# Two norm rows, a few multiplies and four block sums of a decoder layer, moved between engines and in time

## Chip, cores and metric

The kernel runs on all 8 cores of one Trainium2 chip, two dies of four cores. Every core runs the same program on its own part of the tokens. The metric is the device time of the slowest core in microseconds. The three fast executions of the kernel before lie within 0.8 us. In some executions the cores of one die show a lower granted TensorE clock and the time is longer: in one of the kernel before, cores 0 to 3 took 1647.1 to 1666.9 us at mean granted clocks of 0.816 to 0.833, cores 4 to 7 1422.4 to 1428.5 us at 0.993 to 0.995.

## The reference, cut to what matters

```python
def _layer(x, attend_fn, conv_prev, ffn_prev, g_attn_norm, w_in, ..., w_out, g_ffn_norm, w_gate, w_up, ..., w_down):
    ...
    x = x + mixed @ w_out
    h = _rmsnorm(x, g_ffn_norm)                                   # the FFN norm row
    a, ffn_state = _causal_dwconv(h @ w_gate, ffn_prev, ffn_conv_w)
    x = x + (jax.nn.silu(a + ffn_conv_b) * (h @ w_up)) @ w_down
    return x, k, v, conv_state, ffn_state
# after the layer: y = _rmsnorm(x, g_final)                       # the final norm rows
```

A norm row is `rsqrt(mean(x*x) + eps)` over 2048 features. Features lie on partitions here, so the sum is a matmul with a matrix of ones, and the root is `exp(-0.5 * ln(...))` on ScalarE. The gate, up and down products are done as seven block products instead of eight (P1, P2, P6, P5, P7, P3, P4), which needs sums and differences of operand blocks beforehand.

## The kernel before

Three places matter. First, the FFN norm row. Each of 32 row tiles of the output projection is evicted (VectorE adds the matmul's result in PSUM to the tile in SBUF), copied with its gain into the f16 operand, squared, and added to a running sum on GpSimd:

```python
def wo_post(i):
    ...
    T.tt("dve", x2, pair(wbank(i), W), x2, ALU.add)
    T.act(hq[t][...], x2, AF.Copy, scale=col(V_GF + oc))
    if oc == 0:
        T.act(acc2[t][:, :, 0:W], x2, AF.Square)
    else:
        sq = sqw[i % 2][:, :, 0:W]
        T.act(sq, x2, AF.Square)
        if oc < 15:
            T.tt("pool", acc2[t][:, :, 0:W], acc2[t][:, :, 0:W], sq, ALU.add)
        else:
            last2[t] = sq
    ...                                   # three held stores are issued from GpSimd's queue here
def r2_calc(t, b):                        # the row of token half t
    for h in range(2):
        T.mm(psb[b + h][:, 0:W], onesf, acc2[t][:, h, 0:W], start=True, stop=False)
        T.mm(psb[b + h][:, 0:W], onesf, last2[t][:, h, :], start=False, stop=True)
    T.act(r, pair(b, W), AF.Ln, bias=epsc, scale=1.0 / D)
    T.act(pair(b, W), r, AF.Exp, scale=-0.5)
def hook0(name, u, used):                 # called after each unit of each product of the first double
    if (name, u) == ("P2", 0):
        r2_calc(1, 2)                     # TensorE needs GpSimd's last sum here
    if (name, u) == ("P6", 1):
        bg.put(hprep(1), 0.75, tag="h1")  # multiplies by the row, all on VectorE
```

The row of the first token half, `r2_calc(0, 0)`, is taken earlier, inside the output projection. A "double" is the seven block products of two column blocks, 112 matmuls in 13.8 us. Second, background work on VectorE is queued with a cost and a delay. The delay counts units, one product of one column block each. The cost (0.36 below) is what one item takes from a credit that each unit refills, so it decides how many items go out between two evictions:

```python
def after_up(p, c):
    bg.flush(("c", p, c))
    gate_mul(p, c)
    if c == 1:
        bg.put(asums(p), 0.36, delay=6, tag=("T", p))   # four block sums of a pair of gated rows
```

Third, the tail. The last down products leave 144 columns of each token half for 16 small products. The norm rows of the columns that are already done (432 per half) are taken before them, and those columns are scaled and stored beside them ("main stores", yt). Then the row of the rest is taken, and 16 "tail stores" (yz) follow:

```python
fin_calc(1, a3[1], last3[1], r3[1], psb[1][:, 0:R3T])    # row of half 1, before the first product
for oc in range(16):
    ...                                                  # 12 matmuls
    if oc == 0:
        fin_calc(0, a3[0], last3[0], r3[0], rps[0])
    T.tt("dve", x3, h2(ps), x3, ALU.add)
    ...                                                  # square on ScalarE
    if oc < 15:
        T.tt("pool" if oc < 13 else "dve", accT, accT, s_, ALU.add)
    if oc < 14:
        fin0(oc)                                         # scale row oc of the done columns, store it
fin_calc(2, accT, s_, a3[0][:, 0:R3W], rT)
fin0(14); fin0(15)
for oc in range(16):
    ...                                                  # multiply by gain and row, on VectorE
    T.dma("sp", yz_d[oc], zb[oc])
```

The softmax here doesn't subtract the row's maximum and nothing guards it: scores larger than these inputs give would overflow.

## Time and profile before

| | before |
|---|---|
| median of 4 executions, one of them slow | 1431.58 us (1430.86 to 1583.1) |
| spans of the profiled execution, fastest and slowest core | 1420.2 and 1430.1 us |
| TensorE busy on the slowest core | 97% |

### The profile page before, as it was taken

To read this page: it belongs to the slowest core of one execution; us is meant where nothing else is said; L and a number is where in the kernel's file an instruction comes from. 1 tells how busy PE (TensorE), PEld (TensorE's weight loads), DVE (VectorE), ACT (ScalarE), POOL (GpSimd) and SP (SyncE) were. 2 spreads that over 40 slices of the span, in tenths; PEclk is the share of its full clock that TensorE was granted. 3 is DMA by queue.
4 is the path that set the end of the run, shared out by engine and by line. 5 is a ranking of instruction groups with operands and counts; after the bars stand their busy time and mean duration, and the time that the engine had idled before them with its cause. 6 is when DMAs were issued, how large, how long until landed. Compare 5 with 4: busy or idle time off the path is not lost.

```text
span 1430.1 us, 27878 instructions; the slowest of 8 cores (1420.2 to 1430.1 us)
## 1 busy us (share of the span) xinstructions
PE 1383.3 (97%) x11362; PEld 1060.8 (74%) x11362; DVE 958.5 (67%) x1608; ACT 592.1 (41%) x1332; POOL 465.0 (33%) x523
## 2 busy tenths in 40 slices
PE   5999999999999999999999999999999999999996
PEld 4777777777777777777777777777777777777454
DVE  3778577887313868866767676676766665566867
ACT  4536665753333335434443433444344222222234
POOL 2002132331332304322232232223224655456445
PEclk9999999999999999999999999999999999999998
DMA  9937633355988915756665654564345988485607
GB/s 205 245 46 114 94 63 59 63 92 95 236 189 187 173 41 112 151 118 143 134 132 129 136 115 104 128 140 87 66 96 130 273 215 192 76 220 114 111 1 265
DMA packets 49201, 189.15 MB, mean 132 GB/s; under 512 B 9584, under 2 KB 16368, under 8 KB 40624
## 3 DMA queue, kind: packets, MB, share of 16 engines
q0 software_dynamic: 21376, 100.39, 42.8%
q1 hardware_dynamic: 27696, 86.98, 18.6%
q8 instruction: 89, 1.46, 0.4%
q14 instruction: 40, 0.33, 0.1%
HBM read 249.42 MB, written 40.77 MB: 203 GB/s over the span
## 4 chain that ended last, share of the span: by engine, by line
PE 81%; DVE 8%; DMA 5%; issue 2%; ACT 2%; POOL 2%; SPq 1%; DVEq 0%; POOLq 0%; ACTq 0%
PE psb L214 81%; DVE arena L239 6%; DMA arena<-xt 2%; DVE arena L258 2%; POOL arena L239 1%; ACT arena L235 1%; DMA arena<-wout 1%; DMA arena<-wg 1%; DMA arena<-wd 1%; SPq L209 1%; DMA x2s<-arena 0%; ACT arena L263 0%; PE psb L218 0%; ACT L235 0%; POOL x2s L209 0%
## 5 line engine op out<-in xcount | busy, mean ns | idle before, releaser
L214 PE MATMUL psb<-arena 128*128 128x288 f16 (+8 forms) x11290 | 1381.7, 284 | 34.2 <-DVE arena L239 14.1
L214 PEld LDWEIGHTS psb<-arena 128*128 128x128 f16 (+2 forms) x11290 | 1056.2, 99 | 354.9 <-issue 22.0
L239 DVE TENSOR_TENSOR arena<-psb,arena 128x288 f32<-128x288 f32 (+11 forms) x756 | 330.2, 455 | 330.7 <-PE psb L214 313.5
L239 POOL TENSOR_TENSOR arena<-arena 128x288 f32<-128x288 f32 (+6 forms) x378 | 389.9, 1054 | 334.4 <-ACT arena L235 215.2
L239 DVE TENSOR_TENSOR arena<-arena 128x1024 f16<-128x1024 f16 (+12 forms) x583 | 427.4, 749 | 63.0 <-ACT arena L235 32.3
L263 ACT COPY arena<-psb 128x289 f32<-128x289 f32 (+4 forms) x624 | 243.1, 407 | 532.6 <-PE psb L214 467.1
L235 ACT ACTIVATE arena<-arena 128x1184 f32<-128x1184 f32 (+17 forms) x358 | 273.3, 794 | 225.0 <-DVE arena L239 183.2
L258 DVE SCALAR_TENSOR_TENSOR arena<-arena 128x1184 f32<-128x1184 f32 (+5 forms) x140 | 181.2, 1307 | 49.9 <-ACT arena L235 47.3
L209 POOL DMA_DIRECT2D arena<-wu x22 | 11.9, 539 | 277.0 <-PE psb L214 261.8
L235 ACT ACTIVATE arena<-psb,arena 128x256 bf16<-128x256 f32 (+7 forms) x157 | 62.4, 482 | 57.1 <-PE psb L214 57.1
L209 POOL DMA_DIRECT2D arena<-win x30 | 16.5, 572 | 178.7 <-PE psb L214 169.8
L209 POOL DMA_DIRECT2D arena<-wg x22 | 12.9, 586 | 89.0 <-PE psb L214 89.0
L251 DVE TENSOR_SCALAR arena<-arena 128x256 f16<-128x256 f32 (+1 forms) x40 | 12.3, 351 | 18.3 <-DMA arena<-xt 18.3
L263 ACT COPY arena<-arena 128x32 f32<-128x32 f32 (+1 forms) x140 | 24.4, 204 | 0.0
L239 DVE TENSOR_TENSOR arena<-arena,psb 128x1156 f16<-128x1156 f16 (+2 forms) x22 | 23.4, 1104 | 0.0
L209 POOL DMA_DIRECT2D arena<-wd x32 | 18.2, 570 | 11.9 <-PE psb L214 11.9
L258 DVE SCALAR_TENSOR_TENSOR arena<-arena,psb 128x432 f32<-128x432 f32 (+1 forms) x33 | 19.2, 612 | 2.3 <-ACT psb L235 2.3
L209 POOL DMA_DIRECT2D arena<-wout x8 | 4.4, 558 | 36.0 <-PE psb L214 36.0
L265 POOL COPY arena<-arena 128x2 f32<-128x2 f32 (+1 forms) x16 | 5.5, 348 | 13.8 <-DVE arena L239 13.7
L218 PE MATMUL psb<-arena 128*128 128x128 f16 (+1 forms) x72 | 6.7, 212 | 0.0
L218 PEld LDWEIGHTS psb<-arena 128*128 128x128 f16 (+1 forms) x72 | 5.2, 97 | 1.3 <-ACT arena L235 0.2
L263 ACT CAST arena<-psb 128x256 f16<-128x256 f32 (+2 forms) x16 | 4.8, 356 | 3.2 <-PE psb L214 3.2
(17 smaller groups left out, 28.6 us busy)
## 6 DMA issues: line engine op xcount, KB each, us to landing
arena<-wg POOLq DMA_DIRECT2D x22, 1024.0 KB, 13.3
arena<-wu POOLq DMA_DIRECT2D x22, 1024.0 KB, 8.9
acs<-arena SPq DMA_DIRECT2D x16, 1008.0 KB, 5.2
arena<-acs SPq DMA_DIRECT2D x16, 1008.0 KB, 27.3
arena<-win POOLq DMA_DIRECT2D x14, 1024.0 KB, 10.4
arena<-wd POOLq DMA_DIRECT2D x16, 768.0 KB, 12.4
arena<-wd POOLq DMA_DIRECT2D x16, 640.0 KB, 8.9
arena<-x2s SPq DMA_DIRECT2D x16, 576.0 KB, 12.6
```

Source lines behind the costliest of these rows:

```text
L209: return self.add(q, lambda: eo.dma_start(out=out, in_=in_), [in_, *after], [out, *wr], dma=q)
L214: return self.add("pe", lambda: nc.tensor.matmul(out, lhsT, rhs, start=start, stop=stop, **kw), [lhsT, rhs], [out])
L218: return self.add("pe", lambda: nc.tensor.transpose(out, in_, ident), [in_, ident], [out])
L235: return self.add("act", lambda: nc.scalar.activation(out=out, in_=in_, func=func, **kw), rd, wr)
L239: return self.add(eng, lambda: eo.tensor_tensor(out=out, in0=in0, in1=in1, op=op), [in0, in1], [out])
L251: return self.add(eng, lambda: eo.tensor_scalar(out=out, in0=in0, scalar1=s1, scalar2=s2, op0=op0, **kw), rd, [out])
L258: return self.add(eng, lambda: eo.scalar_tensor_tensor(out=out, in0=in0, scalar=scalar, in1=in1, op0=op0, op1=op1), rd, [out])
L263: return self.add("act", lambda: nc.scalar.copy(out=out, in_=in_), [in_], [out])
L265: return self.add(eng, lambda: eo.tensor_copy(out=out, in_=in_), [in_], [out])
```

## The change

The intent is to give TensorE a product to do while GpSimd finishes the norm row, to unload VectorE in the first doubles, and to shorten the work behind the last product. The diff, cut to its core:

```diff
-            T.act(hq[t][...], x2, AF.Copy, scale=col(V_GF + oc))
+            hx = lambda: T.act(hq[t][...], x2, AF.Copy, scale=col(V_GF + oc))
+            if oc < 13:
+                hx()
...
+            if oc > 12:
+                hx()                      # rows 13 to 15: square first, copy after
...
+            if t == 1:
+                T.act(r, r, AF.Exp, scale=-0.5)     # a second copy of the row, in SBUF, for GpSimd
...
-            if (name, u) == ("P2", 0):
+            if (name, u) == ("P2", 1):
                 r2_calc(1, 2)
             if (name, u) == ("P6", 1):
-                bg.put(hprep(1), 0.75, tag="h1")
+                for q, k in [(2, 0), (2, 4)]:
+                    hnorm("pool", 1, q, k, k + 4)
+                bg.put(hprep(1), 0.9, tag="h1")
...
-                bg.put(asums(p), 0.36, delay=6, tag=("T", p))
+                bg.put(asums(p), 0.36, delay=22 if p == 1 else 6, tag=("T", p))
...
+        T.act(lnA[:, 0:1], epsc, AF.Ln)             # loads the logarithm's table early
...
-        fin_calc(1, a3[1], last3[1], r3[1], psb[1][:, 0:R3T])
...
             if oc == 0:
-                fin_calc(0, a3[0], last3[0], r3[0], rps[0])
+                fin_calc(1, [a3[1], last3[1]], r3[1], rps[1])    # both rows after the first product
+                fin_calc(0, [a3[0], last3[0]], r3[0], rps[0])
...
+                if oc < 13:
+                    T.tt("pool", accT, accT, sqT[oc % 4], ALU.add)
+            if oc < 10:
+                T.act(h2(zb[oc]), x3, AF.Copy, scale=col(V_GN + oc))
+            if 0 < oc < 15:
+                fin0(fq.pop(0))
+            if oc in (3, 9):
+                fin0(fq.pop(0))
+        fin_calc(2, [accT, sqT[1], sqT[2], sqT[3]], rTs, rT)     # last three squares summed by TensorE
+        T.act(rTs, rTs, AF.Exp, scale=-0.5)
+        for oc in (0, 2, 3, 1, 5, 7, 4, 8, 10, 6, 11, 12, 9, 13, 14, 15):
+            if oc < 10:
+                T.tt("pool" if oc in (1, 4, 6, 9) else "dve", zb[oc], zb[oc], ..., ALU.mult)
+            else:
+                T.stt("dve", h2(zb[oc]), rowt(oc), col(V_GN + oc), h2(rT), ALU.mult, ALU.mult)
```

More of the change, by code (lines that the diff above doesn't have):

```diff
@@ L1361, in wo_post @@
             T.tt("dve", x2, pair(wbank(i), W), x2, ALU.add)
-            T.act(hq[t][:, 2 * (oc // 8):2 * (oc // 8) + 2, oc % 8, 0:W], x2, AF.Copy, scale=col(V_GF + oc))
+            hx = lambda: T.act(hq[t][:, 2 * (oc // 8):2 * (oc // 8) + 2, oc % 8, 0:W], x2, AF.Copy, scale=col(V_GF + oc))
+            if oc < 13:
+                hx()
             if oc == 0:
@@ L1398, in hnorm @@
             v = hq[t][:, q, k0:k1, 0:W]
-            T.tt(eng, v, v, rps[t][:, q % 2].unsqueeze(1).to_broadcast([128, k1 - k0, W]), ALU.mult)
+            r = rps[t] if eng == "dve" else r2[t][:, :, 0:W]
+            T.tt(eng, v, v, r[:, q % 2].unsqueeze(1).to_broadcast([128, k1 - k0, W]), ALU.mult)
         def hsum(t, o_, a_, b_, eng="dve"):
@@ L1406, in hprep @@
         def hprep(t):
-            hn = lambda q: [lambda k=k: hnorm("dve", t, q, k, k + 4) for k in (0, 4)]
+            hn = lambda q: [lambda k=k: hnorm("dve", t, q, k, k + 4) for k in (0, 4)
+                            if t == 0 or (q, k) not in [(2, 0), (2, 4)]]
             return hn(0) + hn(2) + hn(1) + hn(3) + [
@@ L1900, in sq_acc, with fin_calc @@
                 T.tt("pool", a3[h], a3[h], s_, ALU.add)
-        def fin_calc(bank, acc, last, tmp, out):
-            ps = psb[bank][:, 0:acc.shape[1]]
-            T.mm(ps, onesf, acc, start=True, stop=False)
-            T.mm(ps, onesf, last, start=False, stop=True)
+        def fin_calc(bank, terms, tmp, out):
+            ps = psb[bank][:, 0:tmp.shape[1]]
+            for n, x in enumerate(terms):
+                T.mm(ps, onesf, x, start=(n == 0), stop=(n == len(terms) - 1))
             T.act(tmp, ps, AF.Ln, bias=epsc, scale=1.0 / D)
@@ L1931, in build_nc @@
         R3W = 2 * (576 - R3T)
-        fin_calc(1, a3[1], last3[1], r3[1], psb[1][:, 0:R3T])
-        T.act(r3[1], r3[1], AF.Exp, scale=-0.5)
         rps = [psb[h][:, 0:R3T] for h in range(2)]
@@ L1952, in build_nc, with tail_mm @@
         sqT = [x[:, 0:R3W] for x in (r3[0], sq3[0], sq3[1], sq3[2])]
+        zb = [V((O_P if i < 10 else A_OFF[4] - 10 * 1152) + i * 1152, [R3W]) for i in range(16)]
         def h2(ap):
             return ap.rearrange("p (h c) -> p h c", h=2)
-        for oc in range(16):
+        def tail_mm(oc):
             A = dA(24 + oc // 2)
@@ L1963, in build_nc @@
                 T.mm(ps, A[:, k, c0:c0 + 128], bslt[kk][:, 2 * kh:2 * kh + 2, R3T:576], start=(k == 0), stop=(k == 2 * n3 - 1))
+            return ps
+        fq = list(range(16))
+        for oc in range(16):
+            ps = tail_mm(oc)
             if oc == 0:
-                fin_calc(0, a3[0], last3[0], r3[0], rps[0])
+                fin_calc(1, [a3[1], last3[1]], r3[1], rps[1])
+                fin_calc(0, [a3[0], last3[0]], r3[0], rps[0])
+                T.act(r3[1], r3[1], AF.Exp, scale=-0.5)
             x3 = rowt(oc)
@@ L1970, in build_nc @@
             else:
-                s_ = sqT[oc % 4]
-                T.act(h2(s_), x3, AF.Square)
-                if oc < 15:
-                    T.tt("pool" if oc < 13 else "dve", accT, accT, s_, ALU.add)
-            if oc < 14:
-                fin0(oc)
-        rT = psb[2][:, 0:R3W]
-        fin_calc(2, accT, s_, a3[0][:, 0:R3W], rT)
-        fin0(14)
-        fin0(15)
-        zb = [V((O_P if i < 10 else A_OFF[4] - 10 * 1152) + i * 1152, [R3W]) for i in range(16)]
-        for oc in range(16):
-            if oc % 8 in (2, 5, 7):
-                T.act(h2(zb[oc]), rowt(oc), AF.Copy, scale=col(V_GN + oc))
-                T.tt("dve", zb[oc], zb[oc], rT, ALU.mult)
+                T.act(h2(sqT[oc % 4]), x3, AF.Square)
+                if oc < 13:
[6 more added lines that the diff above has]
+                fin0(fq.pop(0))
+        rT = psb[2][:, 0:R3W]
+        rTs = a3[0][:, 0:R3W]
+        fin_calc(2, [accT, sqT[1], sqT[2], sqT[3]], rTs, rT)
+        T.act(rTs, rTs, AF.Exp, scale=-0.5)
+        for oc in (0, 2, 3, 1, 5, 7, 4, 8, 10, 6, 11, 12, 9, 13, 14, 15):
+            if oc < 10:
+                T.tt("pool" if oc in (1, 4, 6, 9) else "dve", zb[oc], zb[oc], rTs if oc in (1, 4, 6, 9) else rT, ALU.mult)
             else:
```

## The prediction

> **What bounds the kernel now.** I read the page's busy shares first, then the list of cores, then TensorE's own timeline on all eight cores for its idle gaps, then the stretch tables around those gaps, and last the timeline of the final 40 us.
>
> ```profile
> PE 1383.3 (97%) x11362; PEld 1060.8 (74%) x11362; DVE 958.5 (67%) x1608; ACT 592.1 (41%) x1332; POOL 465.0 (33%) x523
> core 3: 1429.4 us, clock 0.994
> core 6: 1430.1 us, clock 0.993
> ```
>
> TensorE is busy 97% of core 6's span, the slowest. A change that leaves the matmuls alone can win only its idle gaps, any time at a low clock, and what comes after its last product. The second slowest core is 0.7 us behind, so a gain on core 6 alone counts only that far.
>
> TensorE's timeline after 470 us, core 6 first, then the two gaps of core 3 (start, duration, and in brackets the idle time before with its releaser):
>
> ```profile
> 488.34 82.51 PE L214 MATMUL psb<-arena 128*128 128x288 f32 x640 [2.01 <-POOL arena L239]
> 571.09 12.06 PE L214 MATMUL psb<-arena 128*128 128x289 f16 x96 [0.24 <-DVE arena L239]
> 584.00 526.00 PE L214 MATMUL psb<-arena 128*128 128x289 f16 x4236 [0.85 <-ACT arena L263]
> 1388.15 26.66 PE L214 MATMUL psb<-arena 128*128 128x432 f32 x200 [0.79 <-DVE arena L239]
> 1415.88 1.60 PE L214 MATMUL psb<-arena 128*128 128x288 f32 x4 [1.07 <-DVE arena L239]
> ...
> 570.07 12.06 PE L214 MATMUL psb<-arena 128*128 128x289 f16 x96 [0.24 <-DVE arena L239]
> 582.99 526.00 PE L214 MATMUL psb<-arena 128*128 128x289 f16 x4236 [0.85 <-ACT arena L263]
> ```
>
> The 2.01 us gap is the FFN norm row waiting for the last square sum on GpSimd. It exists on cores 6 (2.01) and 7 (2.27) only; on cores 0 to 5 VectorE runs level with TensorE there and the row finds its sum ready. The pair 0.24 + 0.85 is on cores 3, 5 and 6 only. The gap of 0.79 and the tail behind it are on all eight. Clock in stretches (the column before the DMA share) just after the first gap, cores 6 and 7:
>
> ```profile
> 488.30:489.50 1.20, 1.16 (x3) 0.91 (x4) 1.20 (x3) 0.00 (x0) 1.20 (x3) 0.50 0.93 337
> 488.00:490.00 2.00, 2.00 (x11) 1.47 (x10) 1.07 (x3) 0.09 (x1) 1.11 (x3) 1.00 1.07 310
> ```
>
> On core 6 the clock is halved after the gap, until about 491.6. On core 7, with a longer gap, it is not. Core 6 needs 676.17 us from 433.82 to 1110 where core 1, with no gap, needs 671.26: 4.9 us, which are 2.01 + 0.24 + 0.85 of gaps and about 1.9 of half clock.
>
> The tail of core 6:
>
> ```profile
> 1413.46 0.46 DVE L239 TENSOR_TENSOR arena<-arena 128x288 f32<-128x288 f32 x1 [1.05 <-POOL arena L239]
> 1415.74 0.45 DVE L239 TENSOR_TENSOR arena<-psb,arena 128x288 f32<-128x288 f32 x1
> 1418.05 0.41 ACT L235 ACTIVATE psb<-arena 128x288 f32<-128x288 f32 x1
> 1424.57 0.45 DVE L239 TENSOR_TENSOR arena<-arena,psb 128x288 f32<-128x288 f32 x1
> 1419.31 8.26 SPq L209 DMA_DIRECT2D yz<-arena  x16
> ```
>
> The last product ends at 1414.81, but VectorE evicts it only at 1415.74, since it had waited 1.05 us for GpSimd's sum. The norm row is ready at 1418.46. VectorE then makes 16 rows by 1425.02, yet SyncE issues the 16 stores one every 0.50 us, the last at 1427.22: VectorE is done 2.2 us before the last issue. The issue of the stores, not the multiplies, sets the end. The list of DMA stretches has 300 to 370 GB/s from 1414 to 1428.
>
> [...]half clock after 2.01 us idle on core 6, none after 2.27 us on core 7, so chance decides at this length. [...]a 128x1024 f16 sum takes 0.68 us alone and 2.10 us beside the GpSimd addition at 486.78, while the PSUM multiplies of the tail keep 0.65 us beside a busy GpSimd.[...]
>
> **Part 1, FFN norm row.** It moves behind one more product of 8 matmuls, 0.99 us of work that fills the gap. The squares of rows 13 to 15 go ahead of the copies, so the square of row 13 is ready 0.67 us earlier; GpSimd's chain (1.85 add, three issues of 0.55, 1.42 add) follows and ends at about 487.55 instead of 488.19. TensorE is free at 486.33 + 0.99 = 487.32. The gap falls from 2.01 to about 0.4, and the half clock should go: 1.6 + 1.9 = 3.5 us on core 6, about 1.8 on core 7, nothing elsewhere. GpSimd takes two multiplies of 1152 elements; from 1.41 us for 576 I estimate 2.8 us each, 5.6 us in all, beside VectorE's own four by then (1.35 each[...]). VectorE loses 2.7 us, but no product waited for it there: worth nothing. The half row is needed about 24 us later.
>
> **Part 2, block sums of pair 1.** Four sums of about 0.45 us leave the double in which a late weight load (13.8 us to landing) has already made VectorE late by 3.5 us. That is 1.8 us of relief against gaps of 0.24 and 0.85 us. I take 0.8 of the 1.09 on cores 3, 5 and 6. The sums land in the next double, where VectorE has some 4 us of room in 14.
>
> **Part 3, the tail.** Products first: TensorE runs 16 products of 1.48 and two norm rows of 1.46 (26.6 us) directly from 1387.36, ends at 1414.02, and gains 0.79 on every core. The table load leaves ScalarE's way, but both rows now come after one product, so the first output multiply starts at about 1395.8 (before: 1394.1). GpSimd does the same 12 additions of 0.80 and 9 multiplies of 1.13, 19.8 us, from about 1395.0 on; its last sum ends near 1414.0 and its last multiply near 1415.1. At the end VectorE has two PSUM multiplies of 0.57 per product, a little over its 1.48, so it evicts the last product at 1414.2. Then 0.45 eviction, 0.45 square, and the four terms of the row: the first three run from 1414.05 to 1415.5 (0.48 each), the last is through at 1416.2, logarithm and exponential 0.95: row ready at 1417.2 instead of 1418.46. The main stores are issued by 1417.0. First tail store at about 1417.75 (before 1419.31), then 15 steps of 0.50 instead of 7.91: last issue 1425.25 instead of 1427.22, 1.95 earlier. The multiplies shared by VectorE and GpSimd buy only the 0.4 of the steps. Against it stands the DMA: from about 1416.5 some 1.33 MB of main stores and 2.36 MB of tail stores are left, 10.2 us at 360 GB/s, so the data end near 1426.8, no sooner than the last issue needs. I take 1.7 us for the tail.
>
> **Sum.** Core 6: 1430.1 - 3.5 - 0.8 - 1.7 = 1424.1. Core 3: 1429.4 - 0.8 - 1.7 = 1426.9. So core 3 becomes the slowest, and the chip gains 3.2 us, not 6. The timed runs stand at 1431.6, so 1431.6 - 3.2 = 1428.4; since some executions will have had a core like 6 in front, I say 1428.2.
>
> **Rivals.** First, the tail stores are bound by DMA bandwidth: moving the main stores later by 1.7 us and together makes a backlog, and the earlier norm row wins nothing. For it: 0.98 to 1.00 DMA share at 1420 to 1424. Against: the last 4 us before fell to 0.84, so the issue had the lead there. Then only 0.8 to 1 us of the tail is left: 1429.2. Second, [...]the weight sums of two SBUF inputs in the first double stretch as the one from 0.68 to 2.10 did, the evictions behind them miss a slack of about 0.55 us, and TensorE gets new gaps of up to 1 us on every core: 1429. Third, the slowest core is decided by the first 60 us, where gaps for input loads differ by 3 us between cores, and a core without the removed gaps leads: gain of the tail alone, 1429.9. Fourth, the executions of before owe their time to the core with gap and half clock, and the chip gains all 6 us: 1425.8.
>
> **Range and chances.** The gains lie between 0.9 and 6 us, and there is no step that could cost more than a microsecond or two. Range 1425.8 to 1430.6. Two per cent are 28 us, more than all idle gaps and the tail together offer, so within 2% gets 0.985; a slow execution among few gives slower 0.01, faster 0.005.
>
> **What would show it.** Right: no gap over 0.6 us before the f32 matmuls near 488 and clock 1.00 behind it; no gap at 571 and 584; none before the norm rows at 1387; the last tail store issued 1.5 to 2.3 us earlier relative to TensorE's last f16 product plus 0.79; store steps of 0.50 from the first on. Wrong: a gap in the first double behind a stretched VectorE sum[...], the stores' issue running well ahead of their landing (bandwidth), or SyncE waiting for GpSimd's last multiply after the row is ready. The prediction fails as a whole if the slowest core loses time in loads that the change does not touch.

3.5 + 0.8 + 1.7 = 6.0 us for core 6, 0.8 + 1.7 = 2.5 us for core 3, so 1430.1 - 1426.9 = 3.2 us for the chip, 1428.4 for the timed runs, put at 1428.2. The 1.28 us of the table load are from the trace (core 6 at 1389.92 us). The 360 GB/s of part 3 are my estimate from stretches like 1419 to 1421 and 1420 to 1422 us, which have 362 and 370. That GpSimd's multiplies would stretch the weight sums (second rival) was my estimate, from the one sum that took 2.10 us beside a GpSimd addition and 0.68 us alone.

## More of the kernel before

To compare kernels I cut each core's span into stages at points that every run has. **Stage 1** runs from TensorE's restart near 432 us, after a short gap that all cores have, to the first eviction of 160 columns on VectorE near 520 us: the end of the output projection, the FFN norm row and the first two doubles. **Stage 2** runs from there to TensorE's restart near 1105 us: the other gate and up products. The **tail stage** runs from TensorE's restart near 1357 us to the end of the span.

## The result, and the profile after

| | before | after |
|---|---|---|
| median of 4 executions | 1431.58 us | 1428.23 us (1426.83 to 1428.63) |
| ratio after / before, fast runs | | 0.9977, 95% interval 0.9957 to 0.9996 |
| spans of the profiled execution, slowest core | 1430.1 us | 1427.6 us |
| the same, mean of the 8 cores | 1425.70 us | 1422.65 us |

The ratio is the mean time of one kernel's fast runs over that of the other's of the same rounds, so not quite the ratio of the medians. Executions in which one die ran at a lower clock are left out of the means. The median of before holds one slow execution; without it, it is 1431.52 us. The gain of 3.3 us is small but outside the noise. By stages, means of the eight cores of the two profiled executions, in us:

| | start to 432 | stage 1 | stage 2 | 1105 to 1357 | tail |
|---|---|---|---|---|---|
| before | 433.32 | 89.23 | 583.80 | 250.91 | 68.44 |
| after | 433.24 | 88.14 | 583.42 | 251.14 | 66.70 |
| difference | -0.08 | -1.09 | -0.38 | +0.23 | -1.74 |

The differences sum to -3.06 and lie in the three stages that the change touches. The cores differ more than that: after, core 3 restarts at 436.78 us and core 6 at 430.74.

The list of cores after:

```profile
core 3: 1427.6 us, clock 0.994
core 6: 1419.3 us, clock 0.996
```

Core 6, which was slowest, is now 8.3 us ahead of core 3. TensorE's timeline after, core 6 first, then core 3 from 440 us on (start, duration, in brackets the idle time before and its releaser):

```profile
430.74 670.56 PE L214 MATMUL psb<-arena 128*128 128x288 f16 x5388 [0.92 <-DVE arena L239]
1352.53 54.06 PE L214 MATMUL psb<-arena 128*128 128x432 f16 x346 [0.47 <-DVE arena L239]
...
571.11 13.04 PE L214 MATMUL psb<-arena 128*128 128x288 f16 x104 [0.48 <-DVE arena L239]
584.32 515.93 PE L214 MATMUL psb<-arena 128*128 128x289 f16 x4154 [0.17 <-DVE arena L239]
```

On core 6 the gap in front of the norm row is gone. One unbroken piece of 670.56 us takes the place of four pieces, and the tail is one piece too, without the gap of 0.79. On core 3 the gaps of 0.24 and 0.85 have become 0.48 and 0.17.

The tail of core 3 after, from the timeline:

```profile
1392.92 0.66 DVE L258 SCALAR_TENSOR_TENSOR arena<-arena,psb 128x432 f32<-128x432 f32 x1
1413.22 0.45 DVE L239 TENSOR_TENSOR arena<-psb,arena 128x288 f32<-128x288 f32 x1
1415.60 0.41 ACT L235 ACTIVATE psb<-arena 128x288 f32<-128x288 f32 x1
1418.24 2.63 DVE L258 SCALAR_TENSOR_TENSOR arena<-arena,psb 128x288 f32<-128x288 f32 x6
1416.63 8.43 SPq L209 DMA_DIRECT2D yz<-arena  x16
```

The tail stage starts 0.67 us earlier here (1360.98) than in core 6 before (1361.65), so add 0.67 to compare. The row is ready at 1416.01 + 0.67 = 1416.68 (before 1418.46). The first tail store is issued at 1417.30 (before 1419.31). VectorE is done at 1420.87 + 0.67 = 1421.54 (before 1425.02). SyncE's last issue is at 1424.72 + 0.67 = 1425.39 (before 1427.22). VectorE gained 3.5 us, the last issue 1.8, and the end of the span 1.7 (mean of all cores).

### The profile page after: what moved, and what is told of

It reads as the page before. It is cut to its first block, busy times and chain, and to the rows that moved or that the text cites. A ratio compares the mean times of both kernels' runs of the same rounds, so it can differ in the third digit from the quotient of the medians.

```text
span 1427.6 us, 27904 instructions; the slowest of 8 cores (1418.7 to 1427.6 us)
## 1 busy us (share of the span) xinstructions
PE 1380.8 (97%) x11366; PEld 1060.1 (74%) x11366; DVE 957.3 (67%) x1600; ACT 594.1 (42%) x1339; POOL 471.1 (33%) x529
## 4 chain that ended last, share of the span: by engine, by line
PE 81%; DMA 8%; DVE 7%; ACT 1%; issue 1%; POOL 1%; SPq 1%; POOLq 0%; DVEq 0%
PE psb L214 80%; DVE arena L239 5%; DMA arena<-xt 3%; DMA arena<-acs 2%; DVE arena L258 1%; DMA arena<-wout 1%; ACT arena L235 1%; DMA arena<-wg 1%; POOL arena L239 1%; SPq L209 1%; DMA arena<-wd 1%; ACT arena L263 0%; PE psb L218 0%; DVE arena L251 0%; ACT L235 0%
## 5 line engine op out<-in xcount | busy, mean ns | idle before, releaser
L239 POOL TENSOR_TENSOR arena<-arena 128x288 f32<-128x288 f32 (+8 forms) x384 | 396.2, 1054 | 338.4 <-ACT arena L235 218.5
L235 ACT ACTIVATE arena<-arena 128x1184 f32<-128x1184 f32 (+18 forms) x365 | 276.1, 788 | 220.1 <-DVE arena L239 175.3
L239 DVE TENSOR_TENSOR arena<-arena,psb 128x1156 f16<-128x1156 f16 (+2 forms) x20 | 20.4, 1081 | 4.5 <-ACT psb L235 4.5
```

The costliest lines, as they stand in the source:

```text
L235: return self.add("act", lambda: nc.scalar.activation(out=out, in_=in_, func=func, **kw), rd, wr)
L239: return self.add(eng, lambda: eo.tensor_tensor(out=out, in0=in0, in1=in1, op=op), [in0, in1], [out])
```

## The experiments

Twelve kernels ran on the chip, all with correct results. "Quiet" is a core whose VectorE is level with TensorE when the norm row comes, "late" one where it is behind.

### The norm row put back

```diff
-            if (name, u) == ("P2", 1):
+            if (name, u) == ("P2", 0):
                 r2_calc(1, 2)
-                ... hnorm("pool", ...) ...     # and the copies in front of the squares for all rows
```

> The changed kernel with the FFN norm row put back (row after the first unit of the second product, copies before squares, no multiply on GpSimd). Stage 1 is TensorE's restart near 432 us to VectorE's first 160-column eviction near 520 us; it took 88.40 us on undisturbed cores, 90.9 and 92.3 on the two with the gap before, 88.14 on all eight after. Theory: only cores where VectorE runs late show it: 88.4 on some, 90 to 92.5 on one to four of the eight, with a gap of about 2 us on GpSimd in front of the f32 matmuls. Rival (the row costs nothing and the gap of before was a chance of that execution): 88.1 to 88.4 on all eight. Tail stage stays at 66.7 +-0.15.

Stage 1 took 88.39 to 92.62 us, mean 89.96. Six of eight cores had the gap: 0.20, 0.74, 1.09, 1.29, 2.15 and 2.33 us. Two of the gaps had the length of about 2 us that I expected on one to four cores. The tail had a mean of 66.85. So the gap is no accident of one execution: with the old row it comes on two cores of eight before and on six here, at a length that changes from core to core and run to run. Core 2's gap in TensorE's timeline, and a stretch of the row behind it (the clock is the column before the DMA share):

```profile
489.85 246.34 PE L214 MATMUL psb<-arena 128*128 128x288 f32 x1960 [2.33 <-POOL arena L239]
```

```profile
491.40:493.00 1.60, 1.60 (x5) 0.87 (x5) 0.00 (x0) 0.18 (x1) 0.00 (x0) 0.50 1.18 138
```

The clock is at 0.50 again, and stage 1 is 92.62 - 88.39 - 2.33 = 1.90 us longer than gap and quiet stage explain. Behind the gap of 1.29 on core 6 the clock stayed at 1.00 and the excess was 0.24; behind the other three short gaps it was 0.23 to 0.24 too. Not expected: stage 2 was about 0.5 us longer than after on quiet cores (583.6 against 583.05), with two gaps of 0.18 waiting for ScalarE near 730 and 841 us. The kernel below with the copies in front of the squares has the same 0.55 us and two such gaps. The edit that both share is the order of copies and squares; how it acts 240 us later is open.

### The gap made longer

```diff
 # in the kernel before
+                    if i == 30:
+                        for _ in range(3):
+                            T.copy("pool", sq, sq)
                     T.tt("pool", acc2[t][:, :, 0:W], acc2[t][:, :, 0:W], sq, ALU.add)
```

> The kernel before with three copies of 576 elements on GpSimd[...] put in front of the last addition of the norm row, so that every core has a gap of some 1 to 5 us in front of the row. Theory: the gap costs more than its length: where it is longer than about 2 us, some or all cores run the eight f32 matmul passes behind it at half clock (0.48 instead of 0.24 us each, 1.9 us in all) and stage 1 is 88.4 + gap + 1.9. Rival (the half clock on core 6 was a chance and not caused by the gap): stage 1 is 88.4 + gap on all cores and the clock in the row is 1.00.

All eight cores had a gap, 2.05 to 3.42 us, and all eight ran at 0.50 behind it. Stage 1 exceeded 88.4 plus the gap by 1.76 to 1.92 us on six cores, and by 3.1 on the two with the gaps of 3.37 and 3.42 us. Core 4's gap, and the stretch behind it:

```profile
492.04 620.54 PE L214 MATMUL psb<-arena 128*128 128x288 f32 x4972 [2.05 <-POOL arena L239]
```

```profile
492.10:493.60 1.50, 1.50 (x4) 1.07 (x5) 0.35 (x1) 0.00 (x0) 1.38 (x3) 0.50 0.45 169
```

In the profiles of the kernel before, of this one and of the one with the row put back there are twelve gaps of 2 us or more in front of the row. Eleven were followed by half clock and one (2.27 us, core 7 before) was not. None of the four gaps up to 1.29 us was. In front of this row, a gap of 2 us with half clock behind it cost about 4 (2.01 and some 1.9 on core 6 before).

Which gap half clock follows is not chance in these profiles, and the traces show what separates the two kinds, though I had overlooked it. A core's clock record in the trace lists when the granted clock changes. On core 6 before it begins at 17.27 us, with changes at 27.51, 30.92, 44.57, 47.99, 488.31 and 491.72 us; the distances are 3, 1, 4, 1, 129 and 1 times 3.413 us. In the records of all cores before and after, each of the 18 stretches at half clock before the tail lasts 3.413 us, and all distances are multiples of it within 0.003 us. So I divided each core's time into steps of this measured length, starting from its own changes, and looked how much of a gap falls into one step. I take the 526 gaps over 0.9 us between 110 and 1395 us, on all cores of all profiles. In eleven of them 1.98 us or more fell into one step, and half clock followed each time. In the other 515 at most 1.91 us did, and it never followed. (The ends of TensorE's records are modelled, so the hundredths are rough.) The share in one step does not explain every half clock: on cores 0 and 3 before it also came at 218.63 and 220.80 us, for 3.413 us each, in the middle of 112.33 us in which TensorE's timeline shows no gap. The 2.27 us of core 7 are cut by the steps into 1.24 and 1.03. Even the 2.58 us of core 5 before, far from the norm row, have at most 1.87 in one step, and the clock behind them stayed at 1.00:

```profile
1170.84 4.34 PE L214 MATMUL psb<-arena 128*128 128x288 f16 x34 [2.58 <-DMA arena<-acs]
1170.84:1172.84 2.00, 2.00 (x17) 1.60 (x18) 0.13 (x1) 0.80 (x2) 0.00 (x0) 1.00 1.03 371
```

### The squares behind the copies again

```diff
-            if oc < 13:
-                hx()
+            hx()
...
-            if oc > 12:
-                hx()
```

> The changed kernel with the norm row still one product on and its GpSimd share, but the squares of rows 13 to 15 behind the copies again. On late cores the changed kernel's relatives show a gap of 0.44 us on GpSimd before the f32 matmuls, the old row 2.0 to 2.3. Theory (the product covers 0.99 us, the earlier squares the rest): a gap of 1.0 to 1.3 us and stage 1 of 89.2 to 89.6 on late cores, no half clock, 88.14 on the others. Rival (the move alone does it): 0.44 us or less on late cores, as with the squares first.

Two cores were late, with gaps of 0.55 and 1.01 us and no half clock. The relatives of the changed kernel that keep the squares in front have 0.35 to 0.45 there on late cores. One gap lies in the expected range of 1.0 to 1.3 and one below it. So, as far as two cores can say, the product in between does most of it, and the earlier squares the rest. The quiet cores showed what I had not foreseen: 88.39 us in place of 88.14. The row of the first token half, inside the output projection, also waited for its last square. The view is VectorE's, ScalarE's and TensorE's load timeline of core 1 near 447 us, before and then after; the f32 load is the row's:

```profile
446.12 0.76 DVE L239 TENSOR_TENSOR arena<-psb,arena 128x578 f32<-128x578 f32 x1 [3.20 <-PE psb L214]
448.45 3.63 PEld L214 LDWEIGHTS psb<-arena 128*128 128x128 f32 x24 [0.45 <-issue]
450.28 0.75 ACT L235 ACTIVATE arena<-psb,arena 128x578 f32<-128x578 f32 x1 [1.94 <-PE psb L214]
```

```profile
447.32 0.76 DVE L239 TENSOR_TENSOR arena<-psb,arena 128x578 f32<-128x578 f32 x1 [3.20 <-PE psb L214]
451.22 0.74 ACT L235 ACTIVATE arena<-psb,arena 128x578 f32<-128x578 f32 x1 [1.63 <-PE psb L214]
```

From the last eviction to the logarithm it is 4.16 us before and 3.90 after, and TensorE's load no longer stops for 0.45 us. That is the 0.25 us.

### The row's multiplies all on VectorE

```diff
-                for q, k in [(2, 0), (2, 4)]:
-                    hnorm("pool", 1, q, k, k + 4)
-                bg.put(hprep(1), 0.9, tag="h1")
+                bg.put(hprep(1), 0.75, tag="h1")
```

> The changed kernel with all FFN row multiplies on VectorE, none on GpSimd, the row still one product on. Theory: VectorE has room, so stage 1 stays at 88.14 +-0.1 on all cores; the GpSimd share gains nothing and costs nothing. Rival (the 0.25 us that stage 1 lost on quiet cores come from VectorE's relief): 88.3 to 88.5. Other rival[...]: stage 1 becomes shorter than 88.1.

None of the three held. Stage 1 took 88.74 us on quiet cores, 0.60 more than after, and all eight cores had a new gap of 0.33 us near 500 us. Late cores took 89.8 to 90.2. VectorE's first multiplies and the eviction behind them on core 3, and TensorE's gap:

```profile
492.21 6.41 DVE L239 TENSOR_TENSOR arena<-arena,psb 128x1152 f16<-128x1152 f16 x5 [1.40 <-ACT psb L235]
498.55 0.45 DVE L239 TENSOR_TENSOR arena<-psb,arena 128x289 f32<-128x289 f32 x1
499.05 4.18 PE L214 MATMUL psb<-arena 128*128 128x289 f16 x32 [0.33 <-DVE arena L239]
```

Five multiplies go in front of the eviction of P7, and P4 has to wait for that bank. As changed only four stand there:

```profile
493.46 5.15 DVE L239 TENSOR_TENSOR arena<-arena,psb 128x1152 f16<-128x1152 f16 x4 [2.15 <-ACT psb L235]
494.23 4.73 POOL L239 TENSOR_TENSOR arena<-arena 128x1152 f16<-128x1152 f16 x2 [4.75 <-ACT arena L235]
498.53 0.45 DVE L239 TENSOR_TENSOR arena<-psb,arena 128x289 f32<-128x289 f32 x1
```

Why this hurts only now follows from the program's order: the unit that now fills the gap in front of the row stood behind it before, and gave VectorE 1 us for the multiplies. Moved in front, it is missing there. With the row put back (above), five stood there too, and quiet cores took 88.39 us without a gap. The 0.60 us are the gap of 0.33 and 0.27 more; the short gaps with the row put back also cost 0.23 to 0.24 us more than their length.

But this run undoes two things: GpSimd's share, and the cost of a multiply in VectorE's queue, 0.75 here and 0.9 as changed. I worked the queue's rule through for both: at 0.75 it sends five multiplies ahead of P7's eviction, at 0.9 four, whether six or eight are waiting. So the higher cost alone keeps the fifth out of the way. All eight multiplies on VectorE at 0.9 were not run, so it is not shown that the GpSimd share is needed.

### The block sums put back

```diff
-                bg.put(asums(p), 0.36, delay=22 if p == 1 else 6, tag=("T", p))
+                bg.put(asums(p), 0.36, delay=6, tag=("T", p))
```

> The changed kernel with the four block sums of pair 1 back at their old place. Stage 2 is the first 160-column eviction near 520 us to TensorE's restart near 1105 us; before 583.35 on quiet cores and 584.50 on cores with the two gaps, after 583.05 and 583.66. Theory: the gaps of 0.24 (VectorE) and 0.85 (ScalarE) are back on the cores whose weight load lands late, and stage 2 is 584.2 to 584.5 there, and 583.3 on the others. Rival (the gaps went because the norm row now leaves VectorE less to do or shifts the loads): stage 2 stays at 583.0 to 583.7. Stage 1 stays 88.14, tail 66.7.

Stage 2 took 583.35 to 583.48 on five cores, 584.10 on one, and 584.49 on two, whose gaps are those of before (0.24 and 0.85). After it was 583.04 to 583.18 and 583.66 to 584.05. The theory held, and the quiet cores gain 0.3 us as well. Which wait that is can't be read from the gaps listed.

### The tail put back

The part of the diff from the early table load on was undone.

> The changed kernel with the tail of the kernel before (norm rows before the first product, no early table load, last sums on VectorE, final multiplies on VectorE only). The tail stage is TensorE's restart near 1357 us to the end of the span: 68.44 before, 66.70 after. Theory: the parts are independent, so 68.4 +-0.15 on every core with the gap of 0.79 back; stages 1 and 2 as after (88.14; 583.0 to 583.7). Rival (some of the tail's gain comes from earlier stages, such as later or earlier loads): a tail between 67 and 68.

The tail took 68.31 to 68.56 us, the gap of 0.79 was back on all cores, and stage 2 was as after. The parts are independent. Two cores were late in stage 1 (89.00 and 89.07 us), with a gap of 0.44 us: this is what the moved row leaves of the 2 us.

### The final multiplies all on VectorE

```diff
-                T.tt("pool" if oc in (1, 4, 6, 9) else "dve", zb[oc], zb[oc], rTs if oc in (1, 4, 6, 9) else rT, ALU.mult)
+                T.tt("dve", zb[oc], zb[oc], rT, ALU.mult)
```

> The changed kernel with all 16 final multiplies on VectorE and none on GpSimd, order unchanged. Theory (the issue of 16 stores at 0.50 us on SyncE sets the end, not the multiplies): VectorE needs 16 x 0.4 = 6.4 us, still faster than 16 stores in 8.1 us, so the tail stays at 66.7 +-0.15 us. Rival (the multiplies set the end, as the split on GpSimd suggests): four multiplies of 0.37 us more, tail 68.0 to 68.2 us.

The tail took 66.73 us on average (after 66.70). The third engine buys nothing: the multiplies were not what the end waited for.

### Fewer issues, and two issuing engines

```diff
 # pairs
-            T.dma("sp", yz_d[oc], zb[oc])                       # 16 times
+            T.dma("sp", yz_d[2 * n:2 * n + 2].rearrange("o p c -> p o c"), V(z, [2, R3W]))   # 8 times
 # two issuers
-            T.dma("sp", yz_d[oc], zb[oc])
+            T.dma("sp" if zn[oc] % 2 == 0 else "act", yz_d[oc], zb[oc])
```

> The changed kernel with the 16 tail stores made 8, two rows in one store, multiplies in plain order with rows 3, 5, 7 and 9 on GpSimd. If the issue on SyncE sets the end, eight issues of about 0.6 us end 3 us sooner; if the DMA engines are full, the data take as long as before (3.7 MB left at about 365 GB/s). Theory: both are near: the tail comes down from 66.7 to 65.0 to 66.0 us and the DMA share is 0.97 or more to the end. Rival 1 (issue alone): 63.5 to 64.5 us. Rival 2 (bandwidth alone): 66.5 to 66.9 us.

> The changed kernel with every other tail store issued from ScalarE's queue, 16 stores as before, same bytes and same packets. Theory: the issue is halved to about 4 us and the DMA engines become the bound: tail 65.0 to 66.0 us. Rival 1 (issue alone sets the end): 62.5 to 64 us. Rival 2 (bandwidth sets the end already): 66.5 to 66.9 us.

Both gave 66.08 us on average, 0.62 less than after and just above the expected 65.0 to 66.0. The last issue came 2.5 us earlier, and the time from it to the end of the span grew from 2.9 us to 4.7 (means of eight cores). Stretches of the DMA on core 1 with pairs (the last two columns are the share and GB/s), then core 3 after:

```profile
1411.40:1413.40 2.00, 0.00 (x0) 0.00 (x0) 0.00 (x0) 0.00 (x0) 0.00 (x0) 0.50 1.09 365
1413.40:1415.40 2.00, 0.00 (x0) 0.00 (x0) 0.00 (x0) 0.00 (x0) 0.00 (x0) 0.50 1.03 347
```

```profile
1422.00:1424.00 2.00, 0.00 (x0) 0.00 (x0) 0.00 (x0) 0.00 (x0) 0.00 (x0) 0.50 0.84 292
1424.00:1426.00 2.00, 0.00 (x0) 0.00 (x0) 0.00 (x0) 0.00 (x0) 0.00 (x0) 0.50 0.86 301
```

With pairs the engines are full to the last 2 us (share 1.09 and 1.03 above). As changed they idle for 15% of the last 4 us (0.84 and 0.86), which is 0.6 us, about the whole gain. Two different cures with the same result, and data that now end long after the last issue, show that behind SyncE's issue, 0.6 us away, stands the DMA bandwidth (365 and 347 GB/s in the stretches with pairs).

### The norm rows first again, and no early table load

```diff
 # rows first
+        fin_calc(1, [a3[1], last3[1]], r3[1], rps[1])
+        fin_calc(0, [a3[0], last3[0]], r3[0], rps[0])
+        T.act(r3[1], r3[1], AF.Exp, scale=-0.5)
         for oc in range(16):                       # and the same three lines out of "if oc == 0"
 # no early load
-        T.act(lnA[:, 0:1], epsc, AF.Ln)
```

> The changed kernel with the two final norm rows put back in front of the first product of the tail, all else as changed. Theory (the end is set by the DMA engines and the issue, which start from the first stores): the gap of 0.79 us is back but the stores start no later than now, so only part of it reaches the end: tail 66.9 to 67.3 us. Rival (as predicted, the 0.79 passes on whole): 67.4 to 67.6 us.

> The changed kernel without the early logarithm, so the table load of 1.28 us is back in front of the final norm rows. It moves the first main stores about 1.2 us later and nothing on TensorE. Theory (stores are DMA bound): tail 67.2 to 68.0 us. Rival (TensorE's last product and the norm row behind it set the end): tail 66.7 to 66.9 us.

In both executions cores 4 and 5 lost about 20 us before 432 us, at mean clocks of 0.974 and 0.975: their 1144 matmuls from about 116 us on took 124.7 us, those of the six others 110.7 to 112.3. What starts it is not shown. So only the six others are read. With the rows first the tail took 67.59 to 67.83, mean 67.68: 1.0 more, and the tail stores start 1.05 us later. My theory of the partly hidden gap fell; the gap of 0.79 passes on whole, with 0.2 more. Without the early load the tail took 67.59 to 67.83: also 1.0 more. There the tail stores start 0.45 later, as TensorE waits 0.16 to 0.20 us for GpSimd's last sum, and the 15 steps between the issues take 8.65 us in place of 8.15. All of that lies in the first step, 1.02 us in place of 0.50. So the load's place is worth as much as the order of the products, and both the row and the pressure on the stores carry it. That it lengthens because the DMA queues are full is an inference; no view shows it directly.

### A version meant to beat both

Pairs, and main stores of rows that VectorE made alone issued ahead of rows that wait for GpSimd:

```diff
+            if oc in (1, 4, 7, 10, 12, 14, 15):
+                yst(oc)
+                while pend and oc != 14:
+                    yst(pend.pop(0))
+            else:
+                while pend:
+                    yst(pend.pop(0))
+                pend.append(oc)
```

> A version to beat both: the changed kernel with eight paired tail stores, and main stores of rows made on VectorE alone issued ahead of rows that wait for GpSimd, so that the DMA engines idle less before the end. Theory (bandwidth is the bound and 2 us of idle DMA lie in the tail): tail 65.3 to 65.9 us against 66.08 with pairs alone and 66.7 as changed; total 1 us under the changed kernel. Rival (the multiply order of SyncE's queue is not what idles the DMA): 66.0 to 66.2 us.

The six undisturbed cores took 66.26 us in the tail, not less than pairs alone (66.08), so the order of the main stores gives nothing. Of four executions two were disturbed (1444 and 1445 us, with two cores at mean clocks of 0.975 to 0.977); the others took 1426.10 and 1426.71. The rounds' interval, 0.9849 to 1.0104 against before, decides nothing at chip level. What stands is that pairs, with or without the new order, have a shorter tail stage than both kernels, by 0.4 to 0.6 us against the changed one.

## Why the prediction was right

**The total.** 1428.2 was predicted and 1428.23 measured. The closeness to the last digit is partly luck: single executions of the changed kernel spread over 1.8 us.

**That a gain on one core counts only up to the next** held. Core 6 lost 10.8 us of span, 3.1 of them before 432 us where nothing was changed; the chip lost 2.5 in the profiles. Core 3 was named as the next slowest at 1426.9 and was it at 1427.6, but with other waits for loads than before, so the name is chance. What is shown is that the place among cores is set mostly before 432 us, where restarts lie 6 us apart.

**Part 1**: 3.5 us were predicted on the late core. The profiled execution of the changed kernel had no late core; as far as its relatives show, that was luck. The five relatives with an unchanged first part and no disturbed core have one or two each, and their stage 1 has a mean of 88.30 to 88.46, not 88.14. In the relatives with an unchanged first part, late cores keep the gap of about 0.4 that was predicted (0.35 to 0.45), and some have another of 0.2 to 0.8 waiting for VectorE 2.6 us in front of it, which was not; undisturbed late cores took 88.7 to 89.8 us there, against 90.9 and 92.3 before. Against core 6 that is 2.5 to 3.6 us, so 3.5 is at the upper end. The half clock of 1.9 us went with it, as said; that "chance decides at this length" was wrong, as the clock records show (1.98 us of the gap in one step on core 6, at most 1.24 on core 7). Two steps failed. "Worth nothing" for VectorE's 2.7 us was wrong in its ground, that no product waited there: with the row moved, P4 waits when five multiplies stand in front of an eviction, for 0.60 us on quiet cores. Whether it takes GpSimd or only the higher cost to avoid this is not separated. And "nothing elsewhere" was wrong by the 0.25 us that the earlier squares give to the first half's row on every core. GpSimd's multiplies took 2.37 us each, not 2.8.

**Part 2**: 0.8 predicted on cores with a late load, 584.50 - 583.66 = 0.84 measured where the shift leaves one gap of 0.17; 0.3 on the others was not predicted. Core 3 shows that a late load can still leave 0.48 in front of it (584.05). So the sign "no gap at 571 and 584" did not come true on four of the eight cores: 0.17 stays on all four, and 0.48 too on one.

**The tail**: 1.7 predicted, 1.74 measured, by a sum whose terms were off and cancelled. The first output multiply was put at 1395.8; it came at 1392.92 + 0.67 = 1393.6, before its old time, since the early table load frees 1.28 us that I had mentioned and not used. The row was ready 0.5 us sooner than said (1416.7, not 1417.2), and the first store with it. The store steps took 8.1 us where I said 7.5, against "0.50 from the first on": the second issue takes 1.00 us. And the backlog on the DMA, for which I took off 0.3, is the bound that stands 0.6 us behind. I had also misread the stretches before, which are not at 300 to 370 GB/s throughout. While the stores waited for the row on core 6, the engines were half idle:

```profile
1417.65:1419.65 2.00, 0.00 (x0) 0.00 (x0) 2.00 (x5) 1.97 (x5) 0.00 (x0) 1.00 0.50 192
```

The step that the end depends on the issue and not on the multiplies held, shown by the experiment with all multiplies on VectorE.

**The rivals.** Bandwidth alone fell as the present bound and stood as the next one. The second rival's gap did not come: GpSimd's two multiplies took 4.7 us and VectorE's multiplies beside them kept the 1.35 us that they took before. But the weight sums that it was about came only as GpSimd's multiplies ended (core 3: 498.90 us, 0.68 long), so what they would have cost each other was not tested. The third and fourth rival put the chip at 1429.9 and 1425.8; the measured 1428.23 lies between, and no experiment separates them further.

## What to carry to other kernels

When a dependent row is moved behind one more product, look at what that product was hiding in its old place: here five multiplies behind the row were one too many in front of an eviction as soon as the product was gone. Ask of a short idle gap of TensorE whether half clock follows it, for that doubled the price of the 2 us here (some 1.9 us more); it followed the eleven gaps of which 1.98 us or more fell into one step of 3.413 us, and none of the 515 others. Before speeding up the last computations of a kernel, check whether the issue of the stores or the DMA bandwidth already sets the end, and judge a change of a few microseconds by stages on all cores, since the slowest core is chosen elsewhere.
